# Sixteen expert pairs: twelve through a DRAM table, four added by one-hot products, and the table read back at the end

## The chip, the cores and the metric

The kernel runs on one core of a Trainium2 chip. Its metric is the device time of one execution in microseconds (us), lower is better. The engines are PE (TensorE, matrix products), ACT (ScalarE), DVE (VectorE), POOL (GpSimd) and SP (which here only issues DMAs); each works through its own instructions in order and waits on semaphores for the others.

## The reference, cut to what matters

Two blocks run one after the other on 512 tokens of 1024 numbers. The change lies in the last step of the second block, a mixture of experts with 32 experts, of which each token uses two:

```python
def hierarchical_moe(h, wg_router, bg_router, we_router, be_router, w_gate, w_up, w_down):
    ...
    gates = jax.nn.one_hot(g_sel, N_GROUPS, dtype=jnp.float32)[:, :, None] * exp_w[:, None, :]
    out = jnp.zeros_like(hf)
    for g in range(N_GROUPS):
        a = jnp.einsum('nd,edf->nef', hf, w_gate[g])
        b = jnp.einsum('nd,edf->nef', hf, w_up[g])
        hid = jax.nn.silu(a) * b * gates[:, g, :, None].astype(hf.dtype)
        out = out + jnp.einsum('nef,efd->nd', hid, w_down[g])
    return out.reshape(B, S, D)
...
x = x + hierarchical_moe(h, ...)
```

Each expert has 1024x256 gate, 1024x256 up and 256x1024 down weights, all float32: 3 MB for one expert, 96 MB for all.

## The kernel before

The kernel computes only the tokens that an expert was chosen for, up to 64 for each expert. Experts go in 16 pairs (0 to 15), one expert on 64 rows of the PE array and its partner on the other 64. For pair r the loop at the end of the program does this:

- **Weights.** SP issues the loads of gate and up (tiles gu, lines 983 and 986, 1 MB each) and of down (dn, lines 999 and 1005) in program order. They go into big buffers that rotate by tag (a16, w16, e8, wr), so a load waits until the pair that used its buffer is done.
- **Rows in.** POOL fetches the pair's 128 token rows by an indirect DMA (fetch_rows, line 1296) from x3d, three pairs ahead. PE turns them (thg, line 1305), DVE scales them into hgT (line 1314; two halves of 128x512).
- **Up.** PE runs 32 products into pgu (line 1321). ACT and DVE make the gated hidden rows sh (lines 1325, 1326).
- **Down.** PE turns sh (thd, line 1336), ACT copies it back (line 1337), PE runs 16 products into two halves pdn.
- **Rows out**, in one of two ways. *Through the table* (a pair r below DIRECT): the halves are copied into a tile yr (ACT line 1350, DVE line 1348; the line of its products is 1345), and POOL scatters the 128 rows by an indirect DMA (line 1351) into a DRAM table yd of 1024 rows: row t holds token t's first expert, row 512 + t its second. *By one-hot products* (the others): the halves are split into yh and yl (ACT line 131, DVE line 132; the line of the products is 1362), DVE makes four one-hot matrices (put, line 1369), PE multiplies them with yh and yl (pad, lines 1375 and 1376, 16 products of 128x512), and DVE adds the eight results to fx, the residual stream in SBUF (line 1377). These products of pair r stand behind the up products of pair r + 1; the last pair's stand behind its own down products, and each finished piece of fx is written to the output (line 1393).

Before, DIRECT is 14: pairs 0 to 13 go through the table, 14 and 15 by products. Behind pair 13 results() reads the table back, 8 DMAs of 512 KB into tiles yt, and DVE adds each to fx (lines 1406 and 1407, 128x1024).

The small tiles hg (three, held throughout), hgT, yr, yh, yl and yt share one ring of eight 4 KB buffers (tag s4), so a new one waits until an older one is done with; for a yr that is the end of its scatter. All scatters write the one table yd, and each waits for the one before it. The order of instructions on each engine is set by a scheduler that runs when the program is built.

Of the kernel before, what the change touches and what calls it, by code (L numbers as in the profile page):

```python
# [4 lines left out]
F32 = mybir.dt.float32  # L5
# [5 lines left out]
OP = mybir.AluOpType  # L11
# [5 lines left out]
D = 1024  # L17
# [32 lines left out]
def ap_of(t, off, dims):  # L50

    return bass.AP(tensor=t.tensor, offset=t.offset + off, ap=[t.ap[0]] + [list(d) for d in dims])
# [9 lines left out]
def program(tc, I, out, sb, ps, dr, dbg, upto):  # L62
    nc = tc.nc
# [8 lines left out]
    def a16(name, dt=F32, shape=(128, 8, 512)):  # L72
        return sb.tile(list(shape), dt, name=name, tag="a16", bufs=6)

    def w2(name, shape=(128, 512), dt=F32, bufs=4):
        return sb.tile(list(shape), dt, name=name, tag="s2", bufs=bufs)

    def s4(name, shape=(128, 2, 512), dt=F32):
        return sb.tile(list(shape), dt, name=name, tag="s4", bufs=8)
# [48 lines left out]
    def split(src, hi, lo, gain=None, eng=None):  # L128

        if gain is None:  # L130
            nc.scalar.activation(hi, src, AF.Copy)  # L131
            (eng or nc.vector).tensor_tensor(lo, src, hi.bitcast(F32), OP.subtract)
        else:
            nc.scalar.activation(hi, src, AF.Copy, scale=gain)
            nc.vector.scalar_tensor_tensor(lo, src, gain, hi.bitcast(F32), OP.mult, OP.subtract)
# [24 lines left out]
    def psm(name):  # L160
        return ps.tile([128, 512], F32, name=name, tag="sm", bufs=3)

    def ptp(name):
        return ps.tile([128, 512], F32, name=name, tag="tp", bufs=2)
# [311 lines left out]
    for c in range(4):  # L476
# [7 lines left out]
        for j in range(2):  # L484
# [10 lines left out]
            t = w2(f"mx{g}", (128, 4, 128))  # L495
            nc.vector.tensor_tensor(t, px.rearrange("p (n t) -> p n t", n=4),
                                    ap_of(bsb, g * 128, [[0, 4], [1, 128]]), OP.add)
            t = t.rearrange("p n t -> p (n t)")
# [114 lines left out]
    for ip in range(2):  # L613
        xt = [s4(f"xr{2 * ip + ii}", (128, D)) for ii in range(2)]
        for ii in range(2):
            i = 2 * ip + ii
# [8 lines left out]
        for ii in range(2):  # L625
            i = 2 * ip + ii
# [351 lines left out]
    def load_gu(e, name, tag="a16", steps=False):  # L978


        gu = sb.tile([128, 2, 8, 256], F32, name=f"gu{name}", tag=tag, bufs=6 if tag == "a16" else 2)
        if name in ("0", "1"):
            fetch = [lambda c=c, w=w: nc.sync.dma_start(gu[:, c], w[e].rearrange("(k p) f -> p k f", p=128))
                     for c, w in enumerate((wge, wue))]
        else:
            fetch = [lambda c=c, w=w: nc.sync.dma_start(gu[:, c].rearrange("p k f -> p (k f)"),
                                                        w[e].rearrange("(p k) f -> p (k f)", p=128))
                     for c, w in enumerate((wge, wue))]
        if steps:
            return gu, fetch  # L990
        for f in fetch:
            f()
        return gu
# [52 lines left out]
    fx = a16("fx", F32, (128, 4, D))  # L1046
# [103 lines left out]
    V_ = nc.vector  # L1150
# [149 lines left out]
    def turn_rows(h, name):  # L1300

        for k0 in range(0, 8, 4):
            tp = ptp(f"thg{name}_{k0}")
            for k in range(4):
                nc.tensor.transpose(tp[:, k * 128:(k + 1) * 128], ap_of(h, k0 + k, [[8, 128]]), ident)
            yield tp
# [22 lines left out]
    def expert_down(sh, ws, src, name, last=False, row=None):  # L1329


        m = 128 // len(ws)
        sa, hd = sh[:, 0:256], sh[:, 256:512].rearrange("p (f t) -> p f t", f=2)
        tp = ptp(f"thd{name}")
        for f in range(2):
            nc.tensor.transpose(tp[:, f * 128:(f + 1) * 128], ap_of(sa, f, [[2, 128]]), ident)
        nc.scalar.activation(hd, tp[:, :256].rearrange("p (f t) -> p f t", f=2), AF.Copy)
        if row is not None:
            yr = s4(f"yr{name}", (128, D))
            for half in range(2):  # L1340
                hs = slice(half * 512, half * 512 + 512)
                po = psm(f"pdn{name}_{half}")
                for f in range(2):
                    for a, (gu, dn) in enumerate(ws):
                        nc.tensor.matmul(po[m * a:m * a + m, :], hd[:, f, m * a:m * a + m], dn[f][:, hs],  # L1345
                                         start=f == 0, stop=f == 1)
                if half:
                    V_.tensor_copy(yr[:, hs], po)  # L1348
                else:
                    nc.scalar.activation(yr[:, hs], po, AF.Copy)  # L1350
            nc.gpsimd.indirect_dma_start(out=yd, out_offset=bass.IndirectOffsetOnAxis(ap=row, axis=0), in_=yr,
                                         in_offset=None, bounds_check=2 * S - 1, oob_is_err=False)
            return None
        yh, yl = s4(f"yh{name}", (128, D), F32R), s4(f"yl{name}", (128, D), F32R)
        put = []

        def down(half):
            hs = slice(half * 512, half * 512 + 512)
            po = psm(f"pdn{name}_{half}")
            for f in range(2):  # L1360
                for a, (gu, dn) in enumerate(ws):
                    nc.tensor.matmul(po[m * a:m * a + m, :], hd[:, f, m * a:m * a + m], dn[f][:, hs],
                                     start=f == 0, stop=f == 1)
            split(po, yh[:, hs], yl[:, hs])

        def where():
            put.append(w2(f"put{name}", dt=F32R))
            for i in range(4):
                V_.tensor_scalar(put[0][:, i * 128:(i + 1) * 128], iota, float(128 * i), src, OP.add, OP.is_equal)

        def add(i, half):
            p = (pmm if half else psm)(f"pad{name}_{i}_{half}")
            hs = slice(half * 512, half * 512 + 512)
            pi = put[0][:, i * 128:(i + 1) * 128]
            nc.tensor.matmul(p, pi, yh[:, hs], start=True, stop=False)
            nc.tensor.matmul(p, pi, yl[:, hs], start=False, stop=True)
            V_.tensor_tensor(fx[:, i, hs], fx[:, i, hs], p, OP.add)

        def add_rows():
            where()  # L1380
            for i in range(4):
                for half in range(2):
                    add(i, half)

        if last:
            where()
            for half in range(2):
                down(half)
            for half in range(2):
                hs = slice(half * 512, half * 512 + 512)  # L1390
                for i in range(4):
                    add(i, half)
                    nc.sync.dma_start(out[0, i * 128:(i + 1) * 128, hs], fx[:, i, hs])
            return None
        for half in range(2):
            down(half)
        return add_rows
# [2 lines left out]

    def results():

        for i in range(4):
            for j in range(2):
                t = s4(f"yt{i}_{j}", (128, D))
                nc.sync.dma_start(t, yd[j * S + i * 128:j * S + (i + 1) * 128, :])
                V_.tensor_tensor(fx[:, i, :], fx[:, i, :], t, OP.add)

    for r in range(1, 4):
        fetch_rows(hg[r % 3], srci[:, r:r + 1])  # L1410
# [15 lines left out]
        V_.tensor_copy(nmi, nmx)  # L1426

    add_rows = None
    DIRECT = 14
    for r in range(16):  # L1430
        es, (gtags, dtags), last = (2 * r, 2 * r + 1), PLACES[r % 3], r == 15
        gu, fetch = [], []
        for e, tag in zip(es, gtags):
            if e < len(gus):
                gu.append(gus[e])
            else:
                t, f = load_gu(e, str(e), tag, True)
                gu.append(t)
                fetch += f
        dn = []  # L1440
        for x, tag in enumerate(dtags):
            d, f = load_dn(es if len(dtags) == 1 else es[x:x + 1], f"{r}_{x}", tag, True)
            dn += d
            fetch += f
        for f in fetch:
            f()
        ws = list(zip(gu, dn))
        rows = turn_rows(hg[r % 3], f"{r}") if r else rows0
        sh = expert_up(rows, grs[:, 1, r:r + 1], grs[:, 0, r:r + 1], ws, f"{r}",
                       None if r else other_lists)  # L1450
        if r and r + 3 < 16:
            fetch_rows(hg[r % 3], srci[:, r + 3:r + 4])
        if add_rows:
            add_rows()
        add_rows = expert_down(sh, ws, srcf[:, r:r + 1], f"{r}", last, row[:, r:r + 1] if r < DIRECT else None)
        if r == DIRECT - 1:
            results()


    nval = nc.values_load(nmi[0:1, 0:1], min_val=0, max_val=S)  # L1460
# [3 lines left out]
    with tc.If(nval > CAP):  # L1464
        with tc.For_i(0, 32, 1) as e:
            ws = [(load_gu(e, "x"), load_dn([e], "x", "w16")[0])]
            ov = w2("ov")
            sel, t, ams = ov[:, 0:32], ov[:, 32:160].rearrange("p (i e) -> p i e", i=4), ov[:, 160:288]
# [47 lines left out]
```

## Time and profile before

| | us |
|---|---|
| median of 3 runs (lowest to highest) | 1351.98 (1351.07 to 1356.47) |
| the profiled execution's own time | 1357.14 |
| its span, first to last instruction | 1355.1 |
| PE busy in the span | 1260.5 (93%) |
| DVE, ACT, POOL busy | 700.7, 486.0, 227.8 |

Times inside the execution are us from the start of its span. [...] Pair 0's up products begin at about 1075, and the last piece of output is written just before 1355. An idle time in square brackets is the time that the engine stood idle before the row, and what ended it.

### The profile page before, as it was taken

The page shows a single profiled execution, that of the slowest core. Times are in us where ns is not written, and L with a number is a line of the kernel's source. Part 1 is how long each engine was busy: PE and PEld are TensorE (multiplying, and loading weights), DVE is VectorE, ACT ScalarE, POOL GpSimd, SP SyncE. Part 2 cuts the span into 40 slices and gives each one's busy share as a digit, 9 for nine tenths or more (in the row PEclk, how much of TensorE's full clock was granted, in tenths as well). Part 3 has the DMA queues.
Part 4 walks back from the last instruction along what each step waited for, and adds up shares of the span by engine and source line. Part 5 has one row for each costly group of instructions (what it writes and reads, how often), then busy time and mean ns, then how long its engine had stood idle before and what let it go on. Part 6 is the DMA issues. An engine that isn't in the chain of part 4 may idle for free. (4 is left out here: it accounts for less than half of the span.)

```text
span 1355.1 us, 20558 instructions
## 1 busy us (share of the span) xinstructions
PE 1260.5 (93%) x8342; PEld 994.9 (73%) x8342; DVE 700.7 (52%) x1291; ACT 486.0 (36%) x839; POOL 227.8 (17%) x270
## 2 busy tenths in 40 slices
PE   6999999999999999999999999889999998988627
PEld 5898989899988888888998869658998733333213
DVE  4558676776642254543555499974456521211134
ACT  4455564546332344332433343355443210100001
POOL 2203021120200000100013655441020210111100
PEclk9999999999999999999999999889999999999959
DMA  6332223221732333335441421331294699999961
GB/s 184 94 95 63 64 63 95 63 69 58 267 121 90 97 94 94 89 113 196 145 128 41 119 61 42 94 113 61 83 371 177 240 407 419 417 417 419 416 238 64
DMA packets 118659, 219.58 MB, mean 162 GB/s; under 512 B 15619, under 2 KB 95235, under 8 KB 107424
## 3 DMA queue, kind: packets, MB, share of 16 engines
q1 hardware_dynamic: 107248, 202.08, 41.9%
q10 hardware_dynamic: 7136, 8.67, 1.9%
q0 software_dynamic: 4176, 7.47, 1.5%
q8 instruction: 68, 1.11, 0.3%
q14 instruction: 31, 0.25, 0.1%
HBM read 206.00 MB, written 19.92 MB: 167 GB/s over the span
## 5 line engine op out<-in xcount | busy, mean ns | idle before, releaser
L1321 PE MATMUL pgu<-gu,hgT 128*64 128x512 f32 x512 | 123.3, 611 | 41.0 <-DVE hgT L1314 36.0
L1321 PEld LDWEIGHTS pgu<-gu,hgT 128*64 128x64 f32 x512 | 40.4, 141 | 111.2 <-issue 70.3
L353 ACT ACTIVATE qk<-G 128x512 f32<-128x512 f32 x112 | 69.1, 665 | 51.6 <-DVE G L343 51.6
L1325 ACT ACTIVATE sh<-pgu,grs 128x256 f32<-128x256 f32 x16 | 7.6, 474 | 187.4 <-PE pgu L1321 187.4
L1326 DVE SCALAR_TENSOR_TENSOR sh<-sh,grs,pgu 128x256 f32<-128x256 f32 x16 | 7.7, 480 | 114.1 <-ACT sh L1325 114.1
L340 DVE TENSOR_TENSOR G<-G,T 128x512 f32<-128x512 f32 x56 | 39.2, 700 | 31.4 <-ACT qk L353 28.6
L1345 PE MATMUL pdn<-dn,sh 128*64 128x512 f32 x224 | 51.2, 598 | 0.3
L304 POOL TENSOR_TENSOR T<-T 128x512 f32<-128x512 f32 (+6 forms) x56 | 37.0, 661 | 42.4 <-DVE T L271 38.6
L1296 POOL DMA_INDIRECT hg<-x3d,srci x15 | 15.4, 1028 | 157.7 <-DVE yr L1348 109.5
L153 PE MATMUL pi<-wi,hT_h 128*128 128x256 f32 x128 | 37.4, 292 | 4.0 <-ACT wi L131 2.4
L343 DVE TENSOR_TENSOR G<-G,T 128x512 f32<-128x512 f32 x56 | 38.8, 693 | 0.0
L1348 DVE COPY yr<-pdn 128x512 f32<-128x512 f32 x14 | 9.7, 692 | 54.3 <-PE pdn L1345 54.3
L154 PE MATMUL pi<-wi,hT_h 128*128 128x256 f32 x128 | 37.4, 292 | 0.0
L155 PE MATMUL pi<-wi,hT_l 128*128 128x256 f32 x128 | 37.0, 289 | 0.0
L153 PE MATMUL pv<-wv,hT_h 128*128 128x256 f32 x128 | 36.8, 288 | 0.0
L155 PE MATMUL pv<-wv,hT_l 128*128 128x256 f32 x128 | 36.7, 286 | 0.0
L154 PE MATMUL pv<-wv,hT_h 128*128 128x256 f32 x128 | 36.5, 285 | 0.0
L154 PE MATMUL pg<-wga,hT_h 128*128 128x256 f32 x128 | 36.5, 285 | 0.0
L153 PE MATMUL pg<-wga,hT_h 128*128 128x256 f32 x128 | 36.4, 285 | 0.0
L155 PE MATMUL pg<-wga,hT_l 128*128 128x256 f32 x128 | 36.2, 283 | 0.0
L1345 PEld LDWEIGHTS pdn<-dn,sh 128*64 128x64 f32 x224 | 14.8, 136 | 27.0 <-issue 24.0
L319 PE MATMUL pl<-qk 128*64 128x64 f32 x896 | 34.3, 225 | 0.0
(553 smaller groups left out, 4029.2 us busy)
## 6 DMA issues: line engine op xcount, KB each, us to landing
gu<-in_expert_w_gate SPq DMA_DIRECT2D x32, 1024.0 KB, 18.7
gu<-in_expert_w_up SPq DMA_DIRECT2D x32, 1024.0 KB, 18.8
dn<-in_expert_w_down SPq DMA_DIRECT2D x27, 1024.0 KB, 19.7
wo_r<-in_w_out SPq DMA_DIRECT2D x16, 512.0 KB, 3.4
wq_r<-in_w_in SPq DMA_DIRECT2D x12, 512.0 KB, 3.9
dn<-in_expert_w_down SPq DMA_DIRECT2D x10, 512.0 KB, 20.5
wi_r<-in_w_in SPq DMA_DIRECT2D x8, 512.0 KB, 4.6
wfb_r<-in_w_in SPq DMA_DIRECT2D x8, 512.0 KB, 4.5
```

The lines of the kernel that those rows point to most:

```text
L153: nc.tensor.matmul(o, ah, bh, start=first, stop=False)
L154: nc.tensor.matmul(o, ah, bl, start=False, stop=False)
L155: nc.tensor.matmul(o, al, bh, start=False, stop=last)
L304: nc.gpsimd.tensor_tensor(ap_of(T, o, [[n2, 2], [1, n2]]), ap_of(T, a, [[sa, 2], [2, n2]]), ap_of(T, a + 1, [[sa, 2], [2, n2]]), OP.mult)
L319: nc.tensor.matmul(p[64 * j:64 * j + 64, c * 64:c * 64 + 64], kt[:, k0:k0 + 64], qt[:, q0:q0 + 64], start=True, stop=True)
L340: nc.vector.tensor_tensor(ap_of(G, 0, [[512, 2], [2 * m, nb], [1, m]]), ap_of(G, 0, [[512, 2], [2 * m, nb], [1, m]]), ap_of(T, a + 1, [[sa ...
L343: nc.vector.tensor_tensor(ap_of(G, 1024 + m, [[512, 2], [2 * m, nb], [1, m]]), ap_of(G, 1024 + m, [[512, 2], [2 * m, nb], [1, m]]), ap_of( ...
L353: nc.scalar.activation(ap_of(qk, a * 512, [[2 * m, nb], [m, 2], [1, m]]), ap_of(G, a * 512, [[2 * m, nb], [1024 + m, 2], [1, m]]), AF.Copy)
L1296: nc.gpsimd.indirect_dma_start(out=h, out_offset=None, in_=x3d, in_offset=bass.IndirectOffsetOnAxis(ap=sidx, axis=0), bounds_check=S - 1, ...
L1321: nc.tensor.matmul(pg[m * a:m * a + m, :], hT_[:, k, m * a:m * a + m], ap_of(gu, k * 256, [[2048, 2], [1, 256]]), start=k == 0, stop=k == 7)
L1345: nc.tensor.matmul(po[m * a:m * a + m, :], hd[:, f, m * a:m * a + m], dn[f][:, hs], start=f == 0, stop=f == 1)
L1348: V_.tensor_copy(yr[:, hs], po)
```

## The change

It sets DIRECT to 12, so that pairs 12 and 13 go by one-hot products too, and only twelve scatters are left. It moves the call of results() from behind pair 13 into the last pair's expert_down, behind its down products and ahead of its one-hot products. The eight reads no longer go into eight tiles of the small ring but into two large buffers of 16 KB a partition, one of tag w16 (table rows of the first experts, yt0) and one of tag a16 (second experts, yt1). Of the eight additions, the four on token blocks 0 and 1 go to POOL, the other four stay on DVE.

```diff
@@ -1386,6 +1386,7 @@
             where()
             for half in range(2):
                 down(half)
+            results()
             for half in range(2):
                 hs = slice(half * 512, half * 512 + 512)
                 for i in range(4):
@@ -1400,11 +1401,13 @@
 
     def results():
 
+        ys = [sb.tile([128, 4, D], F32, name=f"yt{j}", tag=tag, bufs=n)
+              for j, (tag, n) in enumerate((("w16", 2), ("a16", 6)))]
         for i in range(4):
             for j in range(2):
-                t = s4(f"yt{i}_{j}", (128, D))
+                t = ys[j][:, i, :]
                 nc.sync.dma_start(t, yd[j * S + i * 128:j * S + (i + 1) * 128, :])
-                V_.tensor_tensor(fx[:, i, :], fx[:, i, :], t, OP.add)
+                (nc.gpsimd if i < 2 else V_).tensor_tensor(fx[:, i, :], fx[:, i, :], t, OP.add)
 
     for r in range(1, 4):
         fetch_rows(hg[r % 3], srci[:, r:r + 1])
@@ -1426,7 +1429,7 @@
         V_.tensor_copy(nmi, nmx)
 
     add_rows = None
-    DIRECT = 14
+    DIRECT = 12
     for r in range(16):
         es, (gtags, dtags), last = (2 * r, 2 * r + 1), PLACES[r % 3], r == 15
         gu, fetch = [], []
@@ -1453,8 +1456,6 @@
         if add_rows:
             add_rows()
         add_rows = expert_down(sh, ws, srcf[:, r:r + 1], f"{r}", last, row[:, r:r + 1] if r < DIRECT else None)
-        if r == DIRECT - 1:
-            results()
```

Nothing ahead of pair 12's down products moves on any engine. In the three places below the number behind a tile's name is first its pair (hgT13 is pair 13's), then a running number of the tile; in pad12_3_0 it is pair, token block, half. The semaphores DMASW belong to POOL's indirect DMAs.

DVE from pair 12's results to pair 14's rows, before:

```order
L1348 COPY yr12_10811<-pdn12_1_10818 128x512 [waits DVE_49,PE_49]
L1314 TENSOR_TENSOR hgT13_10836<-thg13_0_10837,ffc_8137 128x512 [waits DMASW7_49]
L1326 SCALAR_TENSOR_TENSOR sh13_10866<-sh13_10866,grs_9947,pgu13_10849 128x256 [waits Activation_49]
L1348 COPY yr13_10873<-pdn13_1_10880 128x512 [waits DVE_49,PE_49]
L1407 TENSOR_TENSOR fx_9281<-fx_9281,yt0_0_10889 128x1024 [waits DMAHW5_49,DMAHW1_49]
L1407 TENSOR_TENSOR fx_9281<-fx_9281,yt0_1_10892 128x1024 [waits DMAHW6_49,DVE_49]
L1407 TENSOR_TENSOR fx_9281<-fx_9281,yt1_0_10895 128x1024 [waits DMAHW7_49,DMAHW2_49]
L1407 TENSOR_TENSOR fx_9281<-fx_9281,yt1_1_10898 128x1024 [waits DMAHW0_49,DVE_49]
L1314 TENSOR_TENSOR hgT14_10925<-thg14_0_10926,ffc_8137 128x512 [waits DMASW3_49,DVE_49]
```

And the same stretch with the change:

```order
L132 TENSOR_TENSOR yl12_10812<-pdn12_1_10820,yh12_10811 128x512 [waits Activation_49]
L1314 TENSOR_TENSOR hgT13_10836<-thg13_0_10837,ffc_8137 128x512 [waits DMASW0_49]
L1314 TENSOR_TENSOR hgT13_10836<-thg13_4_10843,ffc_8137 128x512 [waits PE_49]
L1369 TENSOR_SCALAR put12_10869<-csq_71,srcf_9934 128x128 x4
L1326 SCALAR_TENSOR_TENSOR sh13_10866<-sh13_10866,grs_9947,pgu13_10849 128x256 [waits Activation_49]
L1377 TENSOR_TENSOR fx_9281<-fx_9281,pad12_0_0_10874 128x512 [waits DMAHW1_49,PE_49]
...
L1377 TENSOR_TENSOR fx_9281<-fx_9281,pad12_3_1_10902 128x512 [waits PE_49]
L132 TENSOR_TENSOR yl13_10911<-pdn13_0_10912,yh13_10910 128x512 [waits DMASW2_49,DVE_49,Activation_49]
L1314 TENSOR_TENSOR hgT14_10938<-thg14_0_10939,ffc_8137 128x512 [waits DVE_49]
```

The four additions of the table stood ahead of hgT14 and are gone from there. DMASW7 before is the end of pair 8's scatter, DMASW0 now is the end of pair 9's, and DMASW2 is the end of pair 11's: with two more 4 KB tiles for each pair (yh and yl in place of yr) the ring comes round sooner, and hgT13 and yl13 now wait for younger scatters.

DVE at the end, with the change, from the last addition of pair 14's products:

```order
L1377 TENSOR_TENSOR fx_9281<-fx_9281,pad14_3_1_11104 128x512 [waits DVE_49,PE_49]
L1410 TENSOR_TENSOR fx_9281<-fx_9281,yt0_11133 128x1024 [waits DMAHW3_49,DVE_49]
L132 TENSOR_TENSOR yl15_11113<-pdn15_0_11119,yh15_11112 128x512 [waits Activation_49]
L1410 TENSOR_TENSOR fx_9281<-fx_9281,yt0_11133 128x1024 [waits DMAHW4_49,DVE_49]
L1410 TENSOR_TENSOR fx_9281<-fx_9281,yt1_11134 128x1024 [waits DMAHW7_49,DVE_49]
L132 TENSOR_TENSOR yl15_11113<-pdn15_1_11126,yh15_11112 128x512 [waits Activation_49]
L1410 TENSOR_TENSOR fx_9281<-fx_9281,yt1_11134 128x1024 [waits DMAHW0_49,DVE_49]
L1377 TENSOR_TENSOR fx_9281<-fx_9281,pad15_0_0_11151 128x512 [waits PE_49,Pool_49]
```

Four additions of the table now stand ahead of the last pair's eight; POOL's four stand alone at the end of its queue, the first waiting for pair 14's second addition, and the last pair's additions on blocks 0 and 1 wait for them. On SP the eight reads (first the four into yt1, then the four into yt0) still stand behind the last load of weights, as before; the first now waits for pair 11's scatter in place of pair 13's.

## Rows read from the trace of the kernel before

**Rows 1.** Stretches: us, busy time of each engine, granted clock, DMA share, GB/s.
```profile
1288.00:1290.00 2.00, 0.00 (x0) 0.00 (x0) 0.00 (x0) 0.00 (x0) 0.00 (x0) 0.50 0.97 403
1300.00:1310.00 10.00, 0.00 (x0) 0.00 (x0) 3.15 (x3) 0.00 (x0) 0.00 (x0) 0.50 0.70 262
1330.00:1340.00 10.00, 10.00 (x48) 5.08 (x46) 5.32 (x15) 0.86 (x2) 0.00 (x0) 1.00 0.00 0
```
**Rows 2.** The chain that ended last: start, us, what.
```profile
1285.52 7.89 DMA yd<-yr,row
...
1294.25 7.63 DMA yd<-yr,row
...
1303.07 6.14 DMA yt<-yd
```
**Rows 3.** Timeline of POOL: start, us, what, [idle before, and its end].
```profile
1248.07 1.00 POOL L1351 DMA_INDIRECT yd<-yr,row  x1 [0.31 <-issue]
1259.46 1.01 POOL L1351 DMA_INDIRECT yd<-yr,row  x1 [10.39 <-DMA yd<-yr,row]
1268.09 0.97 POOL L1351 DMA_INDIRECT yd<-yr,row  x1 [7.62 <-DMA yd<-yr,row]
1276.85 0.97 POOL L1351 DMA_INDIRECT yd<-yr,row  x1 [7.79 <-ACT sh L1337]
```
**Rows 4.** Timeline of SP, the last loads and the reads.
```profile
1279.16 0.33 SPq L986 DMA_DIRECT2D gu<-in_expert_w_up  x1
1281.89 2.05 SPq L1005 DMA_DIRECT2D dn<-in_expert_w_down  x2
1302.08 8.80 SPq L1406 DMA_DIRECT2D yt<-yd  x8
```
**Rows 5.** Timeline of DVE, pairs 13 to 15.
```profile
1262.85 1.28 DVE L1314 TENSOR_TENSOR hgT<-thg,ffc 128x512 f32<-128x512 f32 x2
1305.74 1.23 DVE L1407 TENSOR_TENSOR fx<-fx,yt 128x1024 f32<-128x1024 f32 x1 [24.46 <-DMA yt<-yd]
1311.85 1.29 DVE L1314 TENSOR_TENSOR hgT<-thg,ffc 128x512 f32<-128x512 f32 x2
1326.72 0.69 DVE L132 TENSOR_TENSOR yl<-pdn,yh 128x512 fp32r<-128x512 f32 x1 [3.72 <-ACT yh L131]
1336.30 4.86 DVE L1377 TENSOR_TENSOR fx<-fx,pad 128x512 f32<-128x512 f32 x8
1344.96 4.26 DVE L1377 TENSOR_TENSOR fx<-fx,pad 128x512 f32<-128x512 f32 x7
```
**Rows 6.** Timeline of PE, pairs 13 to 15.
```profile
1266.21 8.56 PE L1321 MATMUL pgu<-gu,hgT 128*64 128x512 f32 x30 [1.56 <-DMA gu<-in_expert_w_up]
1312.60 9.31 PE L1321 MATMUL pgu<-gu,hgT 128*64 128x512 f32 x32 [31.41 <-DVE hgT L1314]
1323.39 0.61 PE L1305 MATMUL thg<-csq,hg 128*128 128x128 f32 x4
1328.26 7.09 PE L1321 MATMUL pgu<-gu,hgT 128*64 128x512 f32 x32
1339.39 3.65 PE L1362 MATMUL pdn<-dn,sh 128*64 128x512 f32 x16
```
**Rows 7.** DMA issues from 1275 to 1300: KB each, median us to landing.
```profile
dn<-in_expert_w_down SPq DMA_DIRECT2D x2, 1024.0 KB, 19.4
gu<-in_expert_w_up SPq DMA_DIRECT2D x1, 1024.0 KB, 18.7
```
**Rows 8.** Timeline of POOL and DVE at three places earlier in the program.
```profile
888.41 2.34 POOL L132 TENSOR_TENSOR wo<-wo_r,wo 128x1024 fp32r<-128x1024 f32 x1
888.51 2.28 DVE L810 TENSOR_TENSOR pool<-pool,cnt 128x16 f32<-128x16 f32 x1
916.42 2.37 POOL L132 TENSOR_TENSOR wo_L<-wo_r,wo_H 128x1024 fp32r<-128x1024 f32 x1 [2.07 <-ACT wo_H L131]
916.94 0.56 DVE L857 CUSTOM_DVE_ANT_0 pm<-pS,ksc 128x384 f32<-128x384 f32 x1 [1.01 <-PE tP L874]
```

## The prediction

> **What bounds the kernel now.** I read the stretches first, to see where PE, busy 93% of the span, is not busy. From 1281 to 1312.6 it does nothing, at 0.50 of the clock, while the weights are still arriving at 403 GB/s [rows 1]. Then the chain of waits, for what ends that gap: not the weights but the table. The scatters of pairs 12 and 13 run one after the other, 7.89 and 7.63 us, and only behind them come the reads of the table, 6.14 us [rows 2]. Then DVE's timeline, for how the table holds PE: the first addition of a table tile sits at the head of DVE's queue for 24.46 us, and pair 14's rows (hgT) stand behind four of them, until 1311.85 [rows 5]. PE's row for pair 14 names the same: 31.41 us idle, ended by hgT [rows 6]. Last SP and the landings: the weights of pair 15 are issued by 1283.94 and land 18.7 to 19.4 us later [rows 4, 7], so gate and up are there by 1298 and down by about 1303. From pair 13 on, the scatters bound the kernel, not the weights.
>
> **The change, part by part.**
>
> *Pair 13's rows come later.* hgT13 now waits for pair 9's scatter, not pair 8's. POOL's four rows are the scatters of pairs 8 to 11, and each starts when the last has ended, so pair 9's ends at 1268.09 [rows 3]; hgT13 ran at 1262.85 before [rows 5]. Up products follow hgT by 0.75 us (1311.85 to 1312.60 [rows 5, 6]), so pair 13's start at 1268.84. They last between 7.09 us (pair 15) and 9.31 us (pair 14, behind an idle PE) [rows 6]; PE will have stood idle for some 6 us, so I take 9.31: they end at 1278.15, against 1274.77 before. A loss of 3.4 us, 1.2 at least.
>
> *Two pairs more by products.* On each of them the two copies become two splits on ACT and DVE (0.69 us on DVE for one [rows 5]), with four one-hot compares, 16 pad products and eight additions (4.86 us [rows 5]). What this is worth on PE is read from pair 15, which already has pair 14's pad products behind its up products: those end at 1335.35, and the down products start at 1339.39, 4.04 us later [rows 6]. For pairs 13 and 14, four transposes of the next rows stand in this stretch (0.61) and four more among the down products (0.61 beside 3.65) [rows 6]. So 4.04 + 0.61 + 3.65 + 0.61 = 8.9 us from the end of one pair's up products to the next pair's, if hgT is there. DVE's eight additions lie beside PE in these 8.9 us and end some 5.8 us in (1341.16 against 1335.35 [rows 5, 6]).
>
> *What takes the place of the 31 us.* hgT14 stands behind yl13, which waits for pair 11's scatter. That one starts at 1276.85 and pair 12's start shows its end, 1285.52 [rows 2, 3]. One split (0.69) and half of hgT (0.75 to PE) later is 1287.0; PE is free at 1278.15 + 8.9 = 1287.05. They meet, so the wait costs nothing if the scatter keeps its time, and every us that it is late goes to the end. Pair 14's up products then end at 1287.05 + 7.09 = 1294.15, pair 15's 16.0 later, at 1310.15, against 1335.35: **25.2 us gained** there. The weights (1298 and 1303) are in time for both: pair 15's up products start at 1303.05, its down products at 1314.2.
>
> *The reads.* The first needs pair 11's scatter, then they need the buffers of pair 13's weights, free at 1278.15 and, for yt0, 1287. SP has nothing else to do. Each read also takes up the completion semaphore of a DMA eight earlier, so the last two go out only when down has landed, about 1303; with 6.14 us [rows 2] they are there by 1310, ahead of 1316, when DVE first asks for one.
>
> *The end.* Counted from the end of pair 15's up products (call it E), DVE's additions of pair 14 begin at 0.95 and end at 5.8; before, the very last addition ended at 1349.22, which is E + 13.9 [rows 5, 6]. Now four table additions of 1.23 us [rows 5] stand in between on DVE, and POOL has four. A POOL operation of this form takes 2.34 to 2.37 us [rows 8]; I take 2.4. Do they run beside each other? An operation of DVE with two SBUF inputs and 16 columns took 2.28 us beside such a POOL operation and ended with it, while one that read PSUM kept its 0.56 us [rows 8]. The table additions have two SBUF inputs (fx and yt); the splits and the pad additions read PSUM. So I let DVE's table additions and POOL's take turns: POOL 2.2 to 7.0 (two), DVE 8.2, POOL 10.6, DVE 11.8, POOL 14.2, DVE 15.4, then a split 16.1 and the last table addition 17.3. Eight pad additions (4.86) end at E + 22.2. That is 8.3 us more than before. If POOL always went first, it would be 9.1 us more; without any blocking POOL ends at 11.8, DVE's row of four additions and two splits (6.3) at 12.1, and the end is E + 17.0, 3.1 more.
>
> [...]
>
> *Sum.* 1310.15 + 22.2 = 1332.4 for the last addition; what follows it lasts 5.9 us as before (1349.22 to 1355.1). Span 1338.3, that is 16.8 less than 1355.1; own time 1340.3 against 1357.14. The profiled execution lies 5.2 above the median of the runs, so the median goes from 1351.98 to **1335**.
>
> **The rivals.**
>
> *The additions overlap.* POOL and DVE add side by side and the end costs 3.1, not 8.3. For it: other long operations of DVE have not been seen blocked to their end. Against: rows 8. 1330.
>
> *The reads slow the last weights.* From 1285.5 they share the queues with pair 15's loads. Four MB at 403 GB/s [rows 1] are 10.4 us; if they were served first, up would land at 1308.5 in place of 1298, and pair 15 would start up to 6 us late: 1341. [...]
>
> *Slower: PE stays at the lower clock.* Pair 13 now starts behind 6 us of idle PE, and the stretch behind it has waits on DVE and ACT in every pair. The clock was 0.50 where PE stood still [rows 1], and pair 14's first products paid for it (9.31 against 7.09 [rows 6]). If it stayed there from pair 13 to the end, a pair of 16.0 us would take about 31 (14.2 up, 7.3 down, some 9 between), and pair 13 5 more: 35 us lost against the sum, 1370. It decides from about half of that stretch on. Against it: PE was at 1.00 with the same work and the same waits from 1330 to 1340 [rows 1].
>
> *Nothing changes* would need DVE's queue to hold another wait of some 17 us ahead of hgT14; the order shows only that for pair 11's scatter, so it takes a scatter far over the 8.7 us that its rows show [rows 3].
>
> **How the numbers follow.** The forecast has 0.64, the overlap 0.16, the slowed weights 0.11, the lower clock 0.05, the late scatter (no change) 0.04. The range runs from the overlap with pair 13 at 7.09 (1330 - 2.2) less 1.5 for the runs' own spread, 1326, to the slowed weights with POOL first and the upper runs of the spread (1341 + 0.8 + 3.2), 1345. A measurement can tell 0.5%, 6.8 us, from no change. The first three cases are all faster than that: 0.91; no change 0.04; slower 0.05.
>
> **What would show it.** In the profile after: no idle PE of over 7 us behind 1262; hgT13 at about 1268.1, released by a scatter; pair 14's up products at about 1287 and of 7.1 us; pair 15's at about 1303; four POOL additions of about 2.4 us with DVE's table additions waiting between them; the last addition 22 us behind the end of pair 15's up products. Wrong would be: table additions of 1.23 us beside POOL's (then 1330), pair 15's up products released by a DMA of weights (then 1341), or granted clock 0.50 behind 1275.

## The result, and the profile after

The changed kernel takes 1337.36 us (median of four runs, 1333.81 to 1340.91); the kernel before 1354.20 (four runs, 1351.07 to 1356.47: the three given above and one more). The ratio is 0.9877, 95% interval 0.9838 to 0.9916: 1.2% faster. The medians differ by 16.8 us, and the prediction had said 16.8 for its span. That the two agree to a tenth is luck: the interval allows 11 to 22 us, and the second comparison of the same two kernels (e12, below) gave 18.9. The forecast median, 1335, lies 2.4 us low, and 2.2 of that is the fourth run of before, which moved its median.

The profiled execution is the fastest of the four: 1333.81 us, span 1332.0, 23.1 less than the span before. Not all of that is the change. Pair 12's hgT, ahead of which nothing was altered, ran at 1246.51 before and at 1240.75 now: 5.8 us that come from earlier stages and differ from one execution to the next (the last section says where). So I count every time from the start of pair 12's hgT, and call it +x. By that the span ends at +91.25, against +108.59 before: **17.3 us** from the change.

PE, pairs 13 to 15 (timeline; start, us, what, idle before and its end), which answers to [rows 6]:

```profile
1262.31 9.05 PE L1321 MATMUL pgu<-gu,hgT 128*64 128x512 f32 x32 [5.26 <-DVE hgT L1314]
...
1281.76 7.16 PE L1321 MATMUL pgu<-gu,hgT 128*64 128x512 f32 x32 [1.44 <-DVE hgT L1314]
...
1297.71 7.04 PE L1321 MATMUL pgu<-gu,hgT 128*64 128x512 f32 x32
1308.81 3.65 PE L1362 MATMUL pdn<-dn,sh 128*64 128x512 f32 x16
...
1320.13 0.79 PE L1375 MATMUL pad<-yh,put 128*128 128x512 f32 x1 [5.31 <-DVE yl L132]
```

The 31.41 us of idle PE ahead of pair 14 are down to 1.44, pair 13 waits 5.26 us where it waited 1.56, and pair 15's up products end at 1304.75, +64.0 (before +88.84). A new wait stands at the very end: PE's last pad products wait 5.31 us for a split on DVE.

DVE, the same stretch to the end, which answers to [rows 5]:

```profile
1261.57 1.29 DVE L1314 TENSOR_TENSOR hgT<-thg,ffc 128x512 f32<-128x512 f32 x2 [3.76 <-DMA yd<-yr,row]
...
1280.42 0.69 DVE L132 TENSOR_TENSOR yl<-pdn,yh 128x512 fp32r<-128x512 f32 x1 [3.18 <-DMA yd<-yr,row]
...
1305.70 4.86 DVE L1377 TENSOR_TENSOR fx<-fx,pad 128x512 f32<-128x512 f32 x8
1310.48 2.40 DVE L1410 TENSOR_TENSOR fx<-fx,yt 128x1024 f32<-128x1024 f32 x1
1312.80 0.68 DVE L132 TENSOR_TENSOR yl<-pdn,yh 128x512 fp32r<-128x512 f32 x1
1313.40 6.08 DVE L1410 TENSOR_TENSOR fx<-fx,yt 128x1024 f32<-128x1024 f32 x2
1319.40 0.68 DVE L132 TENSOR_TENSOR yl<-pdn,yh 128x512 fp32r<-128x512 f32 x1
1320.00 1.21 DVE L1410 TENSOR_TENSOR fx<-fx,yt 128x1024 f32<-128x1024 f32 x1
1321.13 4.86 DVE L1377 TENSOR_TENSOR fx<-fx,pad 128x512 f32<-128x512 f32 x8
```

The two scatter waits that the order had shown are there, at hgT13 and at yl13. Behind pair 14's eight additions the table additions take 2.40, 6.08 for two, and 1.21. POOL's and SP's rows say why, and answer to [rows 3, 4]:

```profile
1270.99 0.98 POOL L1351 DMA_INDIRECT yd<-yr,row  x1 [7.71 <-DMA yd<-yr,row]
1307.06 11.33 POOL L1410 TENSOR_TENSOR fx<-fx,yt 128x1024 f32<-128x1024 f32 x4 [35.09 <-DVE fx L1377]
1280.35 16.46 SPq L1409 DMA_DIRECT2D yt<-yd  x8
```

One line of the program on both engines (view of the tile yt; ns of one, lowest, median, highest):

```profile
L1410 POOL TENSOR_TENSOR fx<-fx,yt x4: 2359/2860/3364, 1307.1 to 1315.1; 128x1024 f32<-128x1024 f32 x4
L1410 DVE TENSOR_TENSOR fx<-fx,yt x4: 1209/2598/3355, 1310.5 to 1320.0; 128x1024 f32<-128x1024 f32 x4
```

DVE's additions stretch from 1.21 to 3.36 us, POOL's from 2.36 to 3.36: each engine waits for the other. And the stretches, which answer to [rows 1] (us, busy time of PE, PEld, DVE, ACT, POOL, granted TensorE clock as a share of full speed, DMA share, GB/s):

```profile
1290.00:1300.00 10.00, 10.00 (x51) 5.21 (x51) 8.12 (x18) 1.58 (x3) 0.00 (x0) 1.00 0.96 365
1300.00:1305.00 5.00, 5.00 (x25) 1.59 (x21) 0.81 (x5) 0.20 (x1) 0.00 (x0) 1.00 0.41 164
1305.00:1310.00 5.00, 5.00 (x24) 3.35 (x24) 4.70 (x9) 0.66 (x2) 2.94 (x2) 1.00 0.04 12
1318.00:1324.00 6.00, 3.87 (x9) 2.71 (x9) 6.00 (x8) 0.00 (x0) 0.40 (x1) 0.50 0.22 84
```

The clock is at 1.00 from 1290 to 1310, and weights and reads are through by about 1305 (DMA share 0.04 from there): no read is what the additions waited for. From 1318 to 1324, behind the 5.31 us in which PE waited for the split, the clock is at 0.50.

### The profile page after: what moved, and what is told of

The parts are those of the page before. It is cut to its first block, busy times and chain, and to the rows that moved or that the text cites. A ratio compares the mean times of both kernels' runs of the same rounds, so it can differ in the third digit from the quotient of the medians.

```text
span 1332.0 us, 20652 instructions
## 1 busy us (share of the span) xinstructions
PE 1261.2 (95%) x8374; PEld 998.1 (75%) x8374; DVE 714.7 (54%) x1313; ACT 487.1 (37%) x841; POOL 236.0 (18%) x272
## 5 line engine op out<-in xcount | busy, mean ns | idle before, releaser
L1321 PE MATMUL pgu<-gu,hgT 128*64 128x512 f32 x512 | 119.7, 603 | 13.4 <-DVE hgT L1314 10.5
L340 DVE TENSOR_TENSOR G<-G,T 128x512 f32<-128x512 f32 x56 | 39.3, 701 | 31.4 <-ACT qk L353 28.6
L1345 PE MATMUL pdn<-dn,sh 128*64 128x512 f32 x192 | 43.8, 598 | 0.3
L319 PEld LDWEIGHTS pl<-qk 128*64 128x64 f32 x896 | 29.3, 137 | 6.2 <-issue 2.1
## 6 DMA issues: line engine op xcount, KB each, us to landing
gu<-in_expert_w_gate SPq DMA_DIRECT2D x32, 1024.0 KB, 18.1
gu<-in_expert_w_up SPq DMA_DIRECT2D x32, 1024.0 KB, 18.6
dn<-in_expert_w_down SPq DMA_DIRECT2D x27, 1024.0 KB, 20.3
dn<-in_expert_w_down SPq DMA_DIRECT2D x10, 512.0 KB, 18.1
```

The lines of the kernel that those rows point to most:

```text
L319: nc.tensor.matmul(p[64 * j:64 * j + 64, c * 64:c * 64 + 64], kt[:, k0:k0 + 64], qt[:, q0:q0 + 64], start=True, stop=True)
L340: nc.vector.tensor_tensor(ap_of(G, 0, [[512, 2], [2 * m, nb], [1, m]]), ap_of(G, 0, [[512, 2], [2 * m, nb], [1, m]]), ap_of(T, a + 1, [[sa ...
L1321: nc.tensor.matmul(pg[m * a:m * a + m, :], hT_[:, k, m * a:m * a + m], ap_of(gu, k * 256, [[2048, 2], [1, 256]]), start=k == 0, stop=k == 7)
```

## The experiments

The theory: the gain comes from moving the table's additions out of DVE's queue ahead of hgT14; at the end they cost what they cost because POOL and DVE add in turns. The rivals: two scatters fewer bring the gain; POOL's half does hide something. In the table E is the end of pair 15's up products, and the last three columns are counted as above.

| kernel | pairs by table | table additions | E | last addition, behind E | span's end |
|---|---|---|---|---|---|
| before | 14 | behind pair 13 | +88.8 | 13.9 | +108.6 |
| the change | 12 | moved, POOL 4, DVE 4 | +64.0 | 21.2 | +91.3 |
| the same again | 12 | as above | +64.0 | 21.2 | +91.2 |
| e1 | 14 | as above | +60.2 | 21.3 | +87.1 |
| e3 | 12 | DVE 8 | +63.7 | 20.9 | +90.0 |
| e4 | 12 | POOL sums 4, DVE 4 | +65.2 | 18.6 | +89.5 |
| e5 | 12 | DVE 4, POOL's left out | +63.7 | 16.3 | +85.6 |
| e8 | 13 | POOL sums 4, DVE 4 | +59.4 | 20.3 | +85.5 |
| e9 | 14 | POOL sums 4, DVE 4 | +59.0 | 22.5 | +86.9 |
| e10 | 13 | POOL sums 2, DVE 6 | +59.5 | 19.1 | +84.8 |
| e11 | 13 | DVE 8 | +57.5 | 20.9 | +84.6 |

**The move alone** (e1).

```diff
-    DIRECT = 12
+    DIRECT = 14
```

> The change with 14 pairs through the table again: only the call of results() is moved (with its two large buffers and POOL's half). Theory (the moved reads bring the gain; the two more product pairs only cost PE time): hgT14 then waits for pair 9's scatter only, so PE runs through pairs 13 to 15 with gaps of under 7 us, and pair 15's up products end some 5 to 7 us sooner than in the changed kernel, that is about 23 us after pair 13's end instead of 33. The reads now wait for pair 13's scatter and land about 6 us later than pair 15's up products end, so table additions are still going in turns when the last products are there: the last addition some 23 to 25 us behind the end of pair 15's up products in place of 21. Together 3 to 5 us faster than the change, ratio to the kernel before 0.984 to 0.986. Rival (two scatters fewer bring the gain): pairs 14 and 15 still wait for the scatters of pairs 12 and 13; an idle PE of about 15 us behind 1275, and the time lies at or above 1345, 0.994 or more.

Measured: 1334.10 us, ratio 0.9834 (0.9811 to 0.9857); by the table 4.2 us faster than the change, though the intervals of the two ratios overlap. There is no long idle PE: hgT14 follows at once behind pair 13's copy, and pair 15 waits only for its weights. Timelines of DVE and PE:

```profile
1278.99 0.69 DVE L1348 COPY yr<-pdn 128x512 f32<-128x512 f32 x1 [4.73 <-PE pdn L1345]
1279.60 1.28 DVE L1314 TENSOR_TENSOR hgT<-thg,ffc 128x512 f32<-128x512 f32 x2
```
```profile
1280.33 7.61 PE L1321 MATMUL pgu<-gu,hgT 128*64 128x512 f32 x32 [0.75 <-DVE hgT L1314]
...
1296.71 7.05 PE L1321 MATMUL pgu<-gu,hgT 128*64 128x512 f32 x30 [1.35 <-DMA gu<-in_expert_w_up]
```

The rival falls: the move brings 28.6 us at E (88.8 to 60.2), and two scatters fewer take 3.8 of them back (5.0 by e9, below, which is the same up to E). One number of mine was off: the last addition comes at E + 21.3, not 23 to 25. The reads, issued only from 1299.35, found little else under way (DMA share 0.20 from 1295 to 1300) and landed in 6.9 us (median; 15.0 in the change), in time for the additions.

What e1 moves is more than a place in DVE's queue: the eight tiles of the table also leave the small ring ahead of hgT14. In the order of before, hgT14 waits for DMASW3 too, the end of pair 12's scatter, at about 1293.4 [rows 2]; in e1 it ran at 1279.60, before that scatter was issued (1282.32). The additions were the later of the two waits, so they set the 31.41 us; by an estimate from these rows, the wait for the scatter alone would have left some 13 of them. No run takes the two apart.

**Twelve pairs alone** (e2: the kernel before, with nothing moved).

```diff
-    DIRECT = 14
+    DIRECT = 12
```

> The kernel before with 12 pairs through the table and nothing moved: results() stands behind pair 11, with its eight small tiles, all additions on DVE. Theory (what matters is where the table's additions stand in DVE's queue): the first four table additions stand ahead of hgT12 and wait for pair 11's scatter, so PE has the same gap of 30 us and more, now ahead of pair 12 (its up products start at about 1285 to 1294), and four pairs by products of 16 us each follow: pair 15's up products end at 1340 to 1351, the span ends at 1355 to 1371, 0 to 16 us slower than before. Rival (two scatters fewer bring the gain): the table is complete 17 us sooner, so the end comes up to 17 us sooner, at 1338 to 1342.

Measured: 1371.81 us (two runs), ratio 1.0105 (1.0078 to 1.0131), slower, with E at 1350.5 and a span of 1370.0, the upper edge of what I expected. Timelines of PE, DVE and SP:

```profile
1295.88 9.55 PE L1321 MATMUL pgu<-gu,hgT 128*64 128x512 f32 x32 [48.63 <-DVE hgT L1314]
```
```profile
1289.18 2.50 DVE L1407 TENSOR_TENSOR fx<-fx,yt 128x1024 f32<-128x1024 f32 x2 [41.82 <-DMA yt<-yd]
...
1295.13 1.29 DVE L1314 TENSOR_TENSOR hgT<-thg,ffc 128x512 f32<-128x512 f32 x2
```
```profile
1284.76 9.33 SPq L1406 DMA_DIRECT2D yt<-yd  x8
1305.41 0.33 SPq L986 DMA_DIRECT2D gu<-in_expert_w_gate  x1
```

The gap is not shortened: it stands ahead of pair 12 now and is longer (48.63 us). The reads now also stand ahead of loads of weights on SP. Where the reading back stands decides, not the number of scatters.

**Eleven pairs** (e6: the change with DIRECT = 11).

> The change with eleven pairs through the table, so that pairs 11 to 15 go by products. Theory (in the changed kernel the small ring just lets the scatters finish in time; each further pair by products moves a wait to a younger scatter): hgT12 now waits for pair 8's scatter and yl12, ahead of hgT13, for pair 10's. Pair 12's up products start some 13 us later than in the change, pair 13's some 8 us later, and pair 15's end some 5 to 9 us later; the reads come earlier, which is worth nothing. Measured from pair 11's up products, about 7 us slower than the change, some 1342 to 1346. Rival (fewer scatters gain something by themselves, PE's extra work is cheap): the same time as the change within 2 us, or faster.

Measured in one execution: 1344.21 us, as expected; counted from pair 11's hgT, E comes 6.9 us later than in the change and the span ends 6.6 later. The wait is where the ring puts it, at pair 12 (PE's timeline):

```profile
1258.18 8.91 PE L1321 MATMUL pgu<-gu,hgT 128*64 128x512 f32 x32 [12.40 <-DVE hgT L1314]
```

**All additions on DVE** (e3).

```diff
-                (nc.gpsimd if i < 2 else V_).tensor_tensor(fx[:, i, :], fx[:, i, :], t, OP.add)
+                V_.tensor_tensor(fx[:, i, :], fx[:, i, :], t, OP.add)
```

> The change with all eight table additions on DVE, none on POOL. Theory (POOL's and DVE's additions exclude each other, POOL takes about 2.4 us where DVE takes 1.23): eight additions of 1.23 us in a row behind pair 14's, and the last addition at E + 21.9 (E is the end of pair 15's up products), where the change has E + 21.2; the same time within 1.5 us. Rival (POOL's half does hide work): DVE's four more additions cost 4.9 us, E + 26.

Measured in one execution: 1341.88 us, in which pair 12's hgT already ran 9.0 us later than in the change; E + 20.9, 1.0 less than expected. POOL's half of the work hides nothing.

**POOL's additions left out** (e5).

```diff
-                (nc.gpsimd if i < 2 else V_).tensor_tensor(fx[:, i, :], fx[:, i, :], t, OP.add)
+                if i >= 2:
+                    V_.tensor_tensor(fx[:, i, :], fx[:, i, :], t, OP.add)
```

> The change without POOL's four table additions (token blocks 0 and 1 of the output lack the table's part; DVE's four additions on blocks 2 and 3 stay). Theory (DVE's four waited for POOL, two operations of one engine never beside one of the other): each of DVE's four now takes 1.2 us in place of 1.2 to 3.4, the last addition comes at E + 17 in place of E + 21.2, and the run is some 4 us shorter from E on. Rival (DVE's additions into fx are long here for another reason, such as reads still landing): they stay at 2.4 us and more, and the last addition stays near E + 21.

Measured in one execution: 1331.94 us; E + 16.3, 4.9 less than the change, and the tile's view:

```profile
L1411 DVE TENSOR_TENSOR fx<-fx,yt x4: 1222/1224/1228, 1313.8 to 1319.0; 128x1024 f32<-128x1024 f32 x4
```

Same instructions, same operands, no POOL beside them: 1.22 us each in place of up to 3.36. Pair 14's eight additions, which read PSUM, take 4.87 us here and 4.86 beside POOL in the change: those are not touched. With e3: each table addition on DVE costs (20.9 - 16.3) / 4 = 1.15 us, and four of them cost about what POOL's four cost in waiting (4.6 against 4.9 us).

**The changed kernel again** (e12, beside e10 and e11).

> The changed kernel once more, beside the others. The prediction's theory: 17 us less than before in the stretch from pair 12's rows to the end, whatever the earlier stretches do; ratio 0.986 to 0.989; last addition at E + 21.2 with DVE's table additions at up to 3.4 us. A rival (the first profile caught a lucky order of POOL and DVE): the last addition elsewhere than at E + 20.5 to 22.

Measured: 1338.38 us, ratio 0.9853 (0.9827 to 0.9879), and the same to 0.1 us in every column. The tile's view, to be laid beside that of the first execution:

```profile
L1410 POOL TENSOR_TENSOR fx<-fx,yt x4: 2362/2864/3367, 1311.7 to 1319.7; 128x1024 f32<-128x1024 f32 x4
L1410 DVE TENSOR_TENSOR fx<-fx,yt x4: 1209/2598/3355, 1315.1 to 1324.6; 128x1024 f32<-128x1024 f32 x4
```

**POOL sums as the reads land** (e4), and the same with 13 (e8) and 14 pairs (e9) through the table.

```diff
-                t = ys[j][:, i, :]
-                nc.sync.dma_start(t, yd[j * S + i * 128:j * S + (i + 1) * 128, :])
-                (nc.gpsimd if i < 2 else V_).tensor_tensor(fx[:, i, :], fx[:, i, :], t, OP.add)
+                nc.sync.dma_start(ys[j][:, i, :], yd[j * S + i * 128:j * S + (i + 1) * 128, :])
+            nc.gpsimd.tensor_tensor(ys[0][:, i, :], ys[0][:, i, :], ys[1][:, i, :], OP.add)
+            V_.tensor_tensor(fx[:, i, :], fx[:, i, :], ys[0][:, i, :], OP.add)
```

> The change with the table's additions arranged otherwise: POOL adds the second experts' rows to the first experts' as the reads land (four additions, table tile to table tile), and DVE adds the four sums to fx. Theory: the reads land from about 5 us before to 2 us behind E (the end of pair 15's up products), so most of POOL's work lies before DVE has a table addition to make, in a time when DVE's work reads PSUM and is not blocked; DVE then has four additions of 1.23 us, and the last addition comes at E + 17 to 18.5 in place of E + 21.2: 3 to 4 us faster than the change. Rival (POOL's additions block whatever DVE does, or the reads land too late for POOL): E + 20 to 22, the same time as the change.

> Thirteen pairs through the table, results() moved, POOL's additions table tile to table tile as the reads land. Theory: the reads wait for pair 12's scatter, so they start some 9 us sooner than with 14 pairs through the table, land in pairs (first and second experts alternate on SP's queue) and POOL has made at least two of its four sums when DVE asks for the first. Pair 15's up products end 1 to 2 us later than with 14 pairs, counted from pair 12's, and the last addition comes at E + 16.5 to 17.5. 2 to 3 us faster than moving results() alone. Rival (the sums still exclude DVE's additions at the end): E + 19 to 21, no faster than moving results() alone.

> Fourteen pairs through the table, results() moved, POOL's additions table tile to table tile as the reads land. Theory: E as with results() moved alone; the first reads land only some 2 us behind E, so POOL's sums (2.4 us each) run beside DVE's additions of pair 14, which read PSUM, and the last of them ends about E + 12 to 13; the last addition comes at E + 18 to 19 in place of E + 21.3: 2 to 3 us faster than moving results() alone. Rival (what lands so late is summed so late that nothing is saved): E + 21, the same time.

Measured: 1335.04 (ratio 0.9834, 0.9804 to 0.9863), 1331.51 (0.9842, 0.9824 to 0.9861) and 1335.20 (0.9871, 0.9854 to 0.9888). At the end e4 gives E + 18.6, just over what I expected; by the span's end it is only 1.8 us ahead of the change, not 3 to 4, with its E 1.2 us later. For e8 and e9 my theory failed: E + 20.3, as its rival had it, and + 22.5, later still than the rival's + 21. By the span's end e8 is 1.6 us ahead of e1, and e9 is level with it. What decides is how early POOL starts: at E - 1.4 in e4, E + 0.5 in e8, E + 2.7 in e9; in e4 and e8 a read is what it waited for. Whatever POOL has not summed when DVE reaches its first table addition is done in turns again; e8's DVE and POOL:

```profile
1304.62 1.76 DVE L1410 TENSOR_TENSOR fx<-fx,yt 128x1024 f32<-128x1024 f32 x1
...
1307.50 5.48 DVE L1410 TENSOR_TENSOR fx<-fx,yt 128x1024 f32<-128x1024 f32 x2
```
```profile
1300.53 4.76 POOL L1409 TENSOR_TENSOR yt<-yt,yt 128x1024 f32<-128x1024 f32 x2 [19.49 <-DMA yt<-yd]
1305.45 6.45 POOL L1409 TENSOR_TENSOR yt<-yt,yt 128x1024 f32<-128x1024 f32 x2 [0.15 <-DMA yt<-yd]
```

While POOL makes one sum, DVE adds the one before it: they work on different data, and DVE's additions still take up to 3.36 us (the tile's view of e8: 1209, 1982, 3355 ns). It isn't a wait for data. So e8 is faster than the change through its earlier E (4.6 us), hardly through its sums (0.9).

**Two sums on POOL, or none** (e10 and e11, 13 pairs through the table). e10 has, in place of e4's two lines:

```diff
+            if i < 2:
+                nc.gpsimd.tensor_tensor(ys[0][:, i, :], ys[0][:, i, :], ys[1][:, i, :], OP.add)
+            else:
+                V_.tensor_tensor(fx[:, i, :], fx[:, i, :], ys[1][:, i, :], OP.add)
+            V_.tensor_tensor(fx[:, i, :], fx[:, i, :], ys[0][:, i, :], OP.add)
```

and e11 is e3 with DIRECT = 13.

> Thirteen pairs through the table, results() moved; POOL sums only token blocks 0 and 1 (first into second experts' rows), DVE adds those two sums and makes the other four additions itself. Theory (only what POOL finishes before DVE's first table addition is free; of POOL's four sums two were done by E + 5.3, and DVE's first table addition comes at about E + 4.6; a table addition on DVE alone costs 1.15 us at the end, from eight at E + 20.9 and four at E + 16.3): six on DVE, the last addition at E + 18.6 plus up to 0.7 of waiting for POOL's second sum, 1 to 2 us faster than with four sums on POOL (E + 20.3). Rival (the end is set by something else than these additions): E + 20 to 21.

> Thirteen pairs through the table, results() moved, all eight table additions on DVE, POOL none. Theory (POOL's additions hide nothing once DVE has table additions to make): E + 20.9, within 1 us of four sums on POOL (E + 20.3), ratio to the kernel before within 0.001 of that kernel's; about 5 us faster than the change by the earlier E. Rival (POOL's four sums hide two DVE additions or more): E + 22.5 or later here.

Measured: e10 1331.52 us, ratio 0.9815 (0.9798 to 0.9831), E + 19.1; e11 1332.12 us, ratio 0.9815 (0.9787 to 0.9842), E + 20.9. e10's two sums are just done when DVE needs them (POOL's row, and DVE's first table addition, stretched by 0.4):

```profile
1299.43 4.77 POOL L1410 TENSOR_TENSOR yt<-yt,yt 128x1024 f32<-128x1024 f32 x2 [19.55 <-DMA yt<-yd]
```
```profile
1303.67 1.61 DVE L1413 TENSOR_TENSOR fx<-fx,yt 128x1024 f32<-128x1024 f32 x1
...
1306.40 1.21 DVE L1413 TENSOR_TENSOR fx<-fx,yt 128x1024 f32<-128x1024 f32 x1
```

Both end some 6.5 us sooner than the change by the table, and both medians lie 6 to 7 us below that of the change on the same chip (1338.38). By the ratios e10's interval lies beside the change's with an overlap of 0.0004, e11's with one of 0.0015. I had expected e11's ratio within 0.001 of e8's; it is 0.0027 lower, against other runs of before. e11 is the plainest: the move, 13 pairs, nothing on POOL. Their E differ by 1.9 us though the two are the same up to there: in e11 pair 12 did not wait for weights (1.18 us in e10), and pair 13's 30 products took 7.05 us in place of 8.70. So a column of one execution is good to some 2 us where weights are waited for, and the differences of 0.2 us among the last rows tell nothing.

## Why the prediction was right

By its own steps, in times from pair 12's hgT (1246.51 in the prediction's time).

- *Pair 13's rows come later*: held. Up products from +22.3 for 9.31 us predicted, from +21.6 for 9.05 measured.
- *What takes the place of the 31 us*: pair 14's up products at +40.5 predicted, +41.0 measured. The step "They meet, so the wait costs nothing" was off by 1.4 us: PE waited 1.44 for hgT14. Pair 11's scatter released yl13 9.4 us after POOL issued it (1270.99 to 1280.42), where I had read 8.7 from the start of one scatter to the start of the next [rows 2, 3]. It did so in e3, e5 and e12 (9.3) and in e4 (9.1) too. So hgT14 was ready 0.5 us late, and PE was free 1.0 us early, because pair 13 had begun sooner; only the first moves E, which stood at +63.6 predicted, +64.0 measured, 24.8 us gained in place of 25.2.
- *The reads*: in time, as predicted, and pair 15's weights not delayed: its up products started without a wait. By SP's waits a load of weights ended seven of the waits ahead of the reads (5.1 us in all for down, 4.3 each for gate and up), which fits the prediction's reading of the semaphores. The rival of the slowed weights, on which no row of before decides, is out: in the second execution of the changed kernel the last gate and up loads, with the reads queued behind them, landed 18.5 and 18.1 us after their issue (18.3 and 18.2 in the first), no later than up's 18.7 before [rows 7].

DMA issues of that execution from 1262 to 1286 (KB each, median us to landing):

```profile
gu<-in_expert_w_gate SPq DMA_DIRECT2D x2, 1024.0 KB, 18.5
gu<-in_expert_w_up SPq DMA_DIRECT2D x2, 1024.0 KB, 18.1
```

- *The end*: turns, as predicted. The sum was 1 us high: E + 22.2 predicted, 21.2 measured, 7.4 us lost in place of 8.3. POOL began where the sum had it (E + 2.3), and its four ended at E + 13.6 in place of 14.2, DVE's last table addition at E + 16.5 in place of 17.3. The rival of overlapping additions fell here, and e5 and e3 show that it was POOL's additions beside them that stretched DVE's: without those, DVE's took about 1.2 us each, in place of up to 3.36. That POOL also waits for DVE, which the sum took for its turns, stands in no row of before ([rows 8] have POOL at 2.34 and 2.37 us); it was the author's estimate, and is now measured: 2.36 to 3.36 us.
- *The lower clock*: it did not stay. It was 0.50 from 1262 to 1266, with 9.05 us for the one pair behind an idle PE, and 1.00 in the stretches from 1290 to 1310. The sign that the prediction named, 0.50 behind 1275, did show from 1318 to 1324, where PE had waited for DVE; there DVE's last eight additions still follow each other in 4.86 us, so it cost nothing that the rows show. In the kernel before, the idle stretch was not at 0.50 throughout, as the prediction has it: 1.00 from 1281 to 1286, 0.50 from 1288 to 1310. Nothing in the sum hangs on that.

The sum: 25.2 - 8.3 = 16.9 predicted, 24.8 - 7.4 = 17.4 measured, with what follows the last addition at 6.0 us (5.9).

What the prediction had not weighed is that the gain is the move's alone, and that hgT14 had also waited for a scatter through the ring. It costed the two product pairs as part of one path; taken apart, the move gives 28.6 us at E, and going from 14 to 12 pairs through the table costs 3.8 to 5.0.

## What to carry to other kernels

When work that waits for a DMA stands in an engine's queue ahead of what the next stage needs, move that work, and count separately what else the edit does: here the move alone gave more than the whole change. Before giving half of an elementwise job to a second engine, look for a row in which the two run side by side with these kinds of operands; if one stretches to the end of the other, as DVE's table additions did here (1.21 to 3.36 us), count on gaining only from what is finished before the first engine starts its own: here POOL's two early sums brought 1.8 us (E + 19.1 in e10, 20.9 in e11). And count from a point that the edit leaves alone: two executions of the changed kernel differed by 4.6 us ahead of that point, a quarter of the gain.

## What the runs showed that I had not expected

**Where executions differ.** The 5.8 us ahead of pair 12 go with an earlier, untouched stage: the granted clock from 850 to 950, in the first execution of the changed kernel, its second (e12) and the kernel before, in this order:

```profile
850.00:950.00 100.00, 92.20 (x555) 66.78 (x554) 72.11 (x187) 51.49 (x118) 31.88 (x20) 0.97 0.27 86
```
```profile
850.00:950.00 100.00, 92.21 (x530) 66.27 (x530) 69.09 (x182) 49.59 (x116) 31.88 (x20) 0.93 0.27 89
```
```profile
850.00:950.00 100.00, 92.07 (x515) 66.07 (x514) 67.53 (x180) 48.45 (x113) 31.90 (x20) 0.91 0.28 86
```

Pair 12's hgT ran at 1240.75, 1245.34 and 1246.51 in these. With the same 92 us of PE busy in 100, the engine got through 555, 530 and 515 matmuls. The clock there isn't all of it: at the same 0.91, pair 11's hgT ran at 1227.32 in e6 and at 1233.00 in e3. What makes the clock differ there was not tried.

**A longer last scatter.** Pair 11's scatter took 9.1 to 9.4 us from its issue on POOL to yl13 on DVE in five profiles. That it is read at DVE is not the reason: of pair 9's, issued at 1253.57, DVE saw the end 8.0 us later (hgT13 at 1261.57), and POOL's next scatter started 8.75 us later:

```profile
1253.57 1.00 POOL L1351 DMA_INDIRECT yd<-yr,row  x1 [10.27 <-DMA yd<-yr,row]
1262.32 0.97 POOL L1351 DMA_INDIRECT yd<-yr,row  x1 [7.75 <-DVE hgT L1314]
```

Nor is it that it comes last: in e2, where it is the last of twelve too, the first read started 7.3 us after its issue, and in e6 the last of eleven released yl12 after 8.1 us. What made it longer stays open.
